# A one-core hybrid decoder layer: TensorE and the head's loads in program order, auxiliary bursts after counted turns, attention's products two turns behind its transposes

## The chip, the cores and the metric

The kernel runs on one core of one Trainium2 chip. The metric is the device time of one execution in microseconds (us). Before the change the timed runs took 1463.61 us in the median of three (1463.49 to 1464.78).

## The reference

One layer of a Hymba-style decoder on a sequence of 256 tokens of width 2048, all in float32. A normed input goes through one wide projection; its parts feed a Mamba-2 state-space branch (32 heads of 64, four groups of B and C) and a sparse attention branch (16 query heads of 128 over 4 groups of keys and values, with a compressed, a selected and a window part). Both are normed, go through one output projection, and a causal ConvFFN follows.

```python
h = rms_norm(x, mix_norm_w[l])
proj = h @ w_in[l]
z, xbc, dt_raw, q, kc, vc, ksl, vsl, kwn, vwn, gl = jnp.split(proj, split_at, axis=-1)
xbc = jax.nn.silu(causal_depthwise_conv(xbc, ssm_conv_w[l], ssm_conv_b[l]))
...
y_ssm = ssd_chunked(...)      # decay_in * (C B^T), times x * dt
y_ssm = rms_norm(y_ssm * jax.nn.silu(z), ssm_norm_w[l])
y_attn = rms_norm(nsa_attention(...), attn_norm_w[l])
x = x + jnp.concatenate([y_attn, y_ssm], axis=-1) @ w_out[l]
h = rms_norm(x, ffn_norm_w[l])
u = causal_depthwise_conv(h @ w_up[l], ffn_conv_w[l], ffn_conv_b[l])
gate, val = jnp.split(u, 2, axis=-1)
x = x + (jax.nn.silu(gate) * val) @ w_down[l]
return rms_norm(x, final_norm_w)
```

## The kernel before

All tokens fit into two tiles of 128 (NT = 2), so the time goes into passing the weights through TensorE once. The kernel is a list of **steps** of 512 KB of weights. For each step one DMA of the sync queue brings `raw` (L328, four buffers, RAWS); ScalarE rounds it to `whi` (L338); VectorE takes the rest, `wlo` (L344); TensorE then multiplies whi with the high and low part of the activations and wlo with the high part: 16 + 8 matmuls of 256 columns (L368, L372), or 8 + 4 of 512 columns where tokens are the rows (L403, L407). Activations are split in the same way, in `hcat` for the input projection, `ya` and `ys` for the output projection, `hcatf` for the up projection.

The steps run in this order: the input projection (PLAN; the word b is the B of the state space, c its C, dt the step sizes, x its inputs, then the keys and values kc, vc, ks, vs, kw, vw, the queries q and the gate z), the output projection (64 steps), the up projection and the down projection. In the input and up projection each four steps end in a `post`, the evacuation of their two PSUM banks (`u`, L386, multiplies with the root r1 of the norm, spread over the partitions as `gate`). There are four banks for steps and four for everything else.

What else is to be done is written as generators, the **auxiliary** work: the products of B and C (`cb_group`, L517), the transposes of dt (L460) and of xs (`make_xdt`, L547), the state-space heads, the compressed blocks, the four groups of the attention, the splitting of ya and ys, the transposes of x1 (L1024) and its root r2 (`make_r2`, L1051). They wait in one queue, `aux`. After each step the loop gives out a number of **turns** (`tick`): 2 per step for b to x, 1.5 where PLAN names no other rate (R_SSM), 1.45 for q and z. A turn runs the first generator to its next `yield`.

An attention group first makes scores and exponentials, then `norm` scales p on VectorE (L813), `trans` transposes a block of p on TensorE (L835) and copies it out of PSUM as `pt` with a high and a low part (ScalarE L94, VectorE L95), and `pv` multiplies it with v (L852 to L854), or with the compressed v (L848). In the code a product follows the transposes of the next block in the same turn.

What sets the order: calls through `V`, `A` and `T` (VectorE, ScalarE, TensorE) are held in program order only while `pin` is set, which is up to step 6; calls of the sync queue are not held. Everywhere else a scheduler may move an engine's instructions against each other, and it places auxiliary matmuls inside steps. In the head, x comes in four loads between the first raw loads, then the parameters (14 small loads, L238 to L250), then the other raw loads, four buffers in turn. Loads are asked for seven steps ahead (LOADS), weights prepared three steps ahead (AHEAD). Steps 0 to 2 also transpose x and split it; the squares of x, the root and its spreading follow steps 3, 4 and 6. `warm_up` issues matmuls on a tile of ones, WARM = 7 ahead of the first transposes and FILL = 4 ahead of the first step.

Of the kernel before, what the change touches and what calls it, by code (L numbers as in the profile page):

```python
# [10 lines left out]
F32 = mybir.dt.float32  # L11
# [8 lines left out]
NT = 2  # L20
# [22 lines left out]
def hymba_kernel(  # L43
# [34 lines left out]
    class Pinned:  # L78


        def __init__(self, eng):
            self.eng = eng

        def __getattr__(self, name):
            fn = getattr(self.eng, name)
            if not pin:
                return fn
            return lambda *a, **kw: tc.keep_in_program_order(fn(*a, **kw))  # L88

    pin = []  # L90
    V, A, T = Pinned(nc.vector), Pinned(nc.scalar), Pinned(nc.tensor)

# [140 lines left out]
    def load_params():  # L233
        def prow(srcs):
            pt = big(24 + len(prow_specs), [P, P], F32, f"prow{len(prow_specs)}")
            r = 0
            for s_ in srcs:
                nc.sync.dma_start(pt[r:r + s_.shape[0], :], s_)  # L238
# [4 lines left out]
        prow([ssm_conv_w[0].rearrange("j (r c) -> (j r) c", c=P), rows(ssm_conv_b[0])])  # L243
        prow([rows(ssm_norm_w[0]), rows(attn_norm_w[0]), rows(ffn_norm_w[0]), cmp_pos_k[0], cmp_pos_v[0]])
        for j in range(3):
            prow([rows(ffn_conv_w[0, j])])
        prow([rows(ffn_conv_b[0])])
        nc.sync.dma_start(dtb, ssm_dt_bias.rearrange("o h -> h o"))
        nc.sync.dma_start(nA, ssm_a_log.rearrange("o h -> h o"))
        nc.sync.dma_start(drow, ssm_d[0].partition_broadcast(P))  # L250

# [66 lines left out]
    def add_chunk(pieces, nk, ncol, mm, post=None, ticks=2, pre=None):  # L318

        kh = nk // 2  # L320
        for hf in range(2):
            s = Step()

            def load(hf=hf, s=s):
                raw = stage.tile([P, 1024], F32, tag="raw", name="raw", bufs=RAWS)
                s.raw = raw[:, :kh * ncol].rearrange("p (k c) -> p k c", k=kh)
                for dst, src in pieces(s.raw, hf * kh, kh):
                    nc.sync.dma_start(dst, src)  # L328

# [95 lines left out]
    def dt_softplus(t80):  # L425
# [28 lines left out]
        A.dma_start(acum_d, e)  # L454
        yield
        ps = aux_bank()
# [53 lines left out]

    def cb_group(g):
        if g % 2 == 0:
            cbt.append(big(29 + g // 2, [P, 2, 384], F32, f"cbt{g // 2}"))
        for st in range(2):
            ps = aux_bank()
            b_ = bc[g][:, 0, :, st * P:(st + 1) * P]
            T.matmul(ps, b_[:, 0], bc[g][:, 1], start=True, stop=False)  # L517
            T.matmul(ps[:, 256:512], b_[:, 1], bc[g][:, 1, 0], start=False, stop=True)
# [22 lines left out]
    def make_xdt(i):  # L541
        xd = big(16 + i, [P, NT, 512], F32, f"xdt{i}")
        xdt.append(xd)
        for t in range(NT):
            ps = aux_bank()
            for j in range(4):
                T.transpose(ps[:, j * P:(j + 1) * P], xs[i][:, j, t * P:(t + 1) * P], ident)  # L547
# [210 lines left out]
    def attention(g):  # L758
# [127 lines left out]
        yield  # L886
        exps(1, 1)
        yield
# [4 lines left out]
        a1 = trans(0, 1)  # L893
        exps(1, 2)
        yield
        a2 = trans(0, 2)
# [5 lines left out]
        pv(po, 0, 1, a1, True, False)  # L902
        yield
        pv(po, 0, 2, a2, False, False)
        prev = trans(1, 1)
        yield
        pv(po, 0, 0, a0, False, True)
        finish(po, 0)
        place_cmp(1)
        po = aux_bank()  # L910
        for b in (2, 3, 4, 0):
            nxt = trans(1, b)
            pv(po, 1, b - 1 if b else 4, prev, b == 2, False)
            prev = nxt
            yield
        pv(po, 1, 0, prev, False, True)
        finish(po, 1)
        yield
# [73 lines left out]
    def split_attn():  # L992
        rr["a"] = token_rsqrt(lambda t: asq[0][:, t * P:(t + 1) * P], "ra")
        yield
        for k in range(16):
# [6 lines left out]
    def split_ssm():  # L1002
        for k in range(16):
# [3 lines left out]
            if k % 2 == 1:  # L1007
                yield
        rr["s"] = token_rsqrt(lambda t: ssq[0][:, t * P:(t + 1) * P], "rs")
        yield  # L1010
# [5 lines left out]

    def transpose_x1(c):
        for kk in range(4):
            k = 4 * c + kk
# [8 lines left out]
    def wout_evac(c, part):  # L1028
        def evac(t, ps):
            sl = x1[c][:, t]  # L1030
            V.scalar_tensor_tensor(sl, ps, rr[part][:, t:t + 1], sl, op0=ALU.mult, op1=ALU.add)
            if part == "s":
                jk = tmp.tile([P, 512], F32, tag="w512", name="junk", bufs=1)
                A.activation(jk, sl, AF.Square, accum_out=xsq[:, t, c:c + 1])
                if t == 1:
                    aux.append(transpose_x1(c))
                    if c == 3:
                        drain()
                        aux.append(make_r2())
        return evac  # L1040

    r2bc = [None]

    def make_r2():
        tot = const.tile([P, NT], F32, name="x1ss")
        V.tensor_reduce(tot, xsq, axis=AX.X, op=ALU.add)
        r2 = rsqrt_mean(tot, NT, "r2")
        yield
        ps = aux_bank()
# [423 lines left out]
    for i in range(n):  # L1473
# [68 lines left out]
```

## Time and profile before

| | us |
|---|---|
| median of the timed runs | 1463.61 |
| profiled execution | 1462.45 |
| its span | 1460.7 |
| TensorE busy, input projection's start (0 to 40) | 35.53 of 40 |
| TensorE busy, 40 to 100 | 58.13 of 60 |
| TensorE busy, 480 to 500 | 19.32 of 20 |
| TensorE busy, 520 to 540 and 540 to 560 | 19.35 and 19.12 of 20 each |
| TensorE busy, up projection (760 to 1200) | 440.00 of 440 |

The span runs from the first to the last instruction; 1.75 us of the execution lie around it. In the timeline a row is a run of like instructions on one engine: start, length, engine, line and count, then in brackets how long the engine had stood still before it and which instruction let it go on. In the list of waits such times are summed by the pair of lines. L88 is the line of the helper that records pinned instructions, L94 and L95 the lines of `split`; "PEld" is the loading of matmul weights, "SPq" the sync queue.

### The profile page before, as it was taken

To read this page: it belongs to the slowest core of one execution; us is meant where nothing else is said; L and a number is where in the kernel's file an instruction comes from. 1 tells how busy PE (TensorE), PEld (TensorE's weight loads), DVE (VectorE), ACT (ScalarE), POOL (GpSimd) and SP (SyncE) were. 2 spreads that over 40 slices of the span, in tenths; PEclk is the share of its full clock that TensorE was granted. 3 is DMA by queue.
4 is the path that set the end of the run, shared out by engine and by line. 5 is a ranking of instruction groups with operands and counts; after the bars stand their busy time and mean duration, and the time that the engine had idled before them with its cause. 6 is when DMAs were issued, how large, how long until landed. Compare 5 with 4: busy or idle time off the path is not lost.

```text
span 1460.7 us, 26504 instructions
## 1 busy us (share of the span) xinstructions
PE 1440.9 (99%) x10512; PEld 1346.8 (92%) x10512; DVE 1103.5 (76%) x1733; ACT 844.2 (58%) x1281; POOL 3.6 (0%) x19
## 2 busy tenths in 40 slices
PE   8999999999999999999999999999999999999997
PEld 8999999989999998888899999999999998788886
DVE  7899699756898898555476776776767778878777
ACT  6666456555676697444455555555555556555554
POOL 0000000000000000000000000000000000000000
PEclk9999999999999999999999999999999999999999
DMA  8667668775444446566556566666666565565664
GB/s 257 172 199 221 179 201 247 219 233 174 145 148 128 148 156 202 189 189 195 189 176 201 191 192 197 196 193 195 195 191 199 190 194 192 194 212 187 204 200 144
DMA packets 222701, 278.77 MB, mean 191 GB/s; under 512 B 13177, under 2 KB 186865, under 8 KB 222449
## 3 DMA queue, kind: packets, MB, share of 16 engines
q1 hardware_dynamic: 220800, 272.59, 59.6%
q10 hardware_dynamic: 1776, 4.50, 0.9%
q8 instruction: 82, 1.34, 0.4%
q14 instruction: 43, 0.34, 0.1%
HBM read 274.92 MB, written 2.13 MB: 190 GB/s over the span
## 4 chain that ended last, share of the span: by engine, by line
PE 90%; DVE 5%; ACT 3%; issue 1%; DMA 1%; DVEq 0%; ACTq 0%
PE mm L368 36%; PE mm L372 18%; PE mm L403 10%; PE mm L407 5%; PE aux L1142 4%; PE mm L1142 3%; PE aux L1145 2%; PE mm L1145 2%; PE mm L88 1%; DVE wlo L344 1%; DVE wlo L1174 1%; PE aux L1191 1%; PE aux L1190 1%; PE aux L585 1%; PE aux L1192 1%
## 5 line engine op out<-in xcount | busy, mean ns | idle before, releaser
L338 ACT ACTIVATE whi<-raw 128x1024 fp32r<-128x1024 f32 x408 | 431.4, 1058 | 428.3 <-PE mm L368 263.6
L344 DVE TENSOR_TENSOR wlo<-raw,whi 128x1024 fp32r<-128x1024 f32 x408 | 496.8, 1219 | 220.2 <-ACT whi L338 214.6
L368 PE MATMUL mm<-hcatf,whi 128*128 128x256 f32 x2816 | 348.6, 276 | 0.0
L368 PEld LDWEIGHTS mm<-hcatf,whi 128*128 128x128 f32 x2816 | 332.6, 188 | 0.1
L368 PE MATMUL mm<-hcat,whi 128*128 128x256 f32 x2192 | 279.2, 279 | 1.9 <-DVE u L386 1.9
L368 PEld LDWEIGHTS mm<-hcat,whi 128*128 128x128 f32 x2192 | 265.2, 188 | 4.5 <-issue 2.5
L372 PE MATMUL mm<-hcatf,wlo 128*128 128x256 f32 x1408 | 188.2, 276 | 0.0
L372 PEld LDWEIGHTS mm<-hcatf,wlo 128*128 128x128 f32 x1408 | 172.7, 188 | 0.0
L372 PE MATMUL mm<-hcat,wlo 128*128 128x256 f32 x1096 | 148.0, 277 | 0.0
L372 PEld LDWEIGHTS mm<-hcat,wlo 128*128 128x128 f32 x1096 | 135.6, 188 | 0.1
L1168 ACT ACTIVATE whi<-raw 128x1024 fp32r<-128x1024 f32 x88 | 91.6, 1056 | 67.8 <-DVE raw L1223 20.6
L1174 DVE TENSOR_TENSOR wlo<-raw,whi 128x1024 fp32r<-128x1024 f32 x88 | 105.7, 1219 | 13.0 <-ACT whi L1168 11.8
L403 PE MATMUL mm<-whi,ya 128*128 128x512 f32 x256 | 65.5, 394 | 0.0
L386 DVE TENSOR_TENSOR u<-mm,bc 128x256 f32<-128x256 f32 x88 | 37.2, 424 | 36.9 <-PE mm L372 35.7
L1142 PE MATMUL aux<-whi,act 128*128 128x512 f32 x256 | 63.4, 390 | 0.8 <-ACT whi L1168 0.8
L403 PE MATMUL mm<-whi,ys 128*128 128x512 f32 x256 | 63.2, 389 | 0.0
L1142 PE MATMUL mm<-whi,act 128*128 128x512 f32 x232 | 58.4, 389 | 0.0
L1142 PEld LDWEIGHTS aux<-whi,act 128*128 128x128 f32 x256 | 47.9, 188 | 11.2 <-ACT whi L1168 1.3
L403 PEld LDWEIGHTS mm<-whi,ys 128*128 128x128 f32 x256 | 48.1, 188 | 10.0
L403 PEld LDWEIGHTS mm<-whi,ya 128*128 128x128 f32 x256 | 47.3, 188 | 9.3
L1142 PEld LDWEIGHTS mm<-whi,act 128*128 128x128 f32 x232 | 43.6, 188 | 9.0
L799 ACT ACTIVATE p<-p,nm 128x256 f32<-128x256 f32 (+2 forms) x96 | 37.7, 394 | 3.0 <-DVE nm L783 1.4
(392 smaller groups left out, 1690.7 us busy)
## 6 DMA issues: line engine op xcount, KB each, us to landing
raw<-in_w_up_dram SPq DMA_DIRECT2D x176, 512.0 KB, 4.5
raw<-in_w_in_dram SPq DMA_DIRECT2D x160, 512.0 KB, 3.7
raw<-in_w_down_dram SPq DMA_DIRECT2D x88, 512.0 KB, 5.0
raw<-in_w_out_dram SPq DMA_DIRECT2D x64, 512.0 KB, 4.8
acq<-acum_d ACTq DMA_DIRECT2D x8, 512.0 KB, 4.7
raw<-in_cmp_w_k_dram SPq DMA_DIRECT2D x8, 512.0 KB, 4.4
raw<-in_cmp_w_v_dram SPq DMA_DIRECT2D x8, 512.0 KB, 4.4
x<-in_x_dram SPq DMA_DIRECT2D x4, 512.0 KB, 6.6
```

Of the source, the lines that this page charges most:

```text
L338: A.activation(hv, s.raw, AF.Copy)
L344: V.tensor_tensor(lv, s.raw, s.w[0].bitcast(F32), op=ALU.subtract)
L368: T.matmul(st["ps"][c], hv[:, kl, c * P:(c + 1) * P], k_of(k)[:, hl], start=(k == 0 and hl == 0), stop=False)
L372: T.matmul(st["ps"][c], lv[:, kl, c * P:(c + 1) * P], k_of(k)[:, 0], start=False, stop=(k == nk - 1))
L386: V.tensor_tensor(u, ps, root, op=ALU.mult)
L403: T.matmul(st["ps"][t], act(k)[:, hl, t * P:(t + 1) * P], hv[:, kl], start=(k == 0 and hl == 0), stop=False)
L407: T.matmul(st["ps"][t], act(k)[:, 0, t * P:(t + 1) * P], lv[:, kl], start=False, stop=(k == nk - 1))
L799: A.activation(v_, v_, AF.Exp, bias=nm[t][:, h, b:b + 1], accum_out=sm[t][:, h, b:b + 1])
L1142: T.matmul(x_[2 * t + n], act(k)[:, hl, t * P:(t + 1) * P], hv[:, n], start=(first and kl == 0 and hl == 0), stop=False)
L1145: T.matmul(x_[2 * t + n], act(k)[:, 0, t * P:(t + 1) * P], lv[:, n], start=False, stop=(last and kl == 1))
L1168: A.activation(hv[:, 0:n], src()[:, 0:n], AF.Copy)
L1174: V.tensor_tensor(lv[:, 0:n], src()[:, 0:n], s.w[0].bitcast(F32)[:, 0:n], op=ALU.subtract)
```

## The change

TensorE is always held in program order (`T` with `always=True`), and the sync queue's raw and parameter loads while `pin` is set, which now begins ahead of the parameters. The parameter loads become a generator that is dealt out between raw loads 4 to 7. FILL is 2. The squares and the root of x both follow step 3, the root is spread after step 5, ahead of the parameters' transposes.

With program order, the place of a burst is where the code issues it, so the code moves them: `pause` lets a generator give back a counted number of turns first (WAIT). `cb_pair` issues the products of two groups as one burst; `make_xdt` all eight transposes at once; the attention keeps transposed blocks in `held` and takes their product two turns later. The root of the attention norm is taken inside `split_ssm` instead of at the start of `split_attn`; the root of x1 at the last evacuation of the output projection, and what is left in `aux` is drained three steps into the up projection instead of at that evacuation. R_SSM goes from 1.5 to 1.75 and the rate of q and z from 1.45 to 1.55.

```diff
-AHEAD, LOADS, WARM, FILL = 3, 7, 7, 4
+AHEAD, LOADS, WARM, FILL = 3, 7, 7, 2
-R_SSM = 1.5
-RATE = {"b": 2, "c": 2, "dt": 2, "x": 2, "ck": 1, "cv": 1, "q": 1.45, "z": 1.45}
+R_SSM = 1.75
+RATE = {"b": 2, "c": 2, "dt": 2, "x": 2, "ck": 1, "cv": 1, "q": 1.55, "z": 1.55}
+WAIT = {"bc": 7, "xdt": 6, "dt": 9, "x1": 2}
...
-            if not pin:
+            if not (pin or self.always):
...
-    V, A, T = Pinned(nc.vector), Pinned(nc.scalar), Pinned(nc.tensor)
+    V, A, T, S = Pinned(nc.vector), Pinned(nc.scalar), Pinned(nc.tensor, True), Pinned(nc.sync)
...
-                    nc.sync.dma_start(dst, src)
+                    S.dma_start(dst, src)
...
         A.dma_start(acum_d, e)
-        yield
+        yield from pause(WAIT["dt"])
...
+    def pause(n):
+        for _ in range(n):
+            yield
+
+    def cb_pair(g0):
+        yield from pause(WAIT["bc"])
+        cbt.append(big(29 + g0 // 2, [P, 2, 384], F32, f"cbt{g0 // 2}"))
+        todo = []
+        for g in (g0, g0 + 1):
+            for st in range(2):
+                ps = aux_bank()
+                b_ = bc[g][:, 0, :, st * P:(st + 1) * P]
+                T.matmul(ps, b_[:, 0], bc[g][:, 1], start=True, stop=False)
+                T.matmul(ps[:, 256:512], b_[:, 1], bc[g][:, 1, 0], start=False, stop=True)
+                todo.append((g, st, ps))
+        for g, st, ps in todo:
...
-            if which == 1:
-                aux.append(cb_group(g))
+            if which == 1 and c == 1:
+                aux.append(cb_pair(g0))
...
-        for t in range(NT):
-            ps = aux_bank()
+        yield from pause(WAIT["xdt"] if i < 3 else WAIT["xdt"] - 1)
+        banks = [aux_bank() for _ in range(NT)]
+        for t, ps in enumerate(banks):
             for j in range(4):
                 T.transpose(ps[:, j * P:(j + 1) * P], xs[i][:, j, t * P:(t + 1) * P], ident)
+        for t, ps in enumerate(banks):
...
+        held = deque()
+
+        def turn(t, blk_):
+            held.append((t, blk_, trans(t, blk_)))
+
+        def product():
+            t, blk_, r = held.popleft()
+            first = blk_ == 1
+            if first:
+                pos[t] = aux_bank()
+            pv(pos[t], t, blk_, r, first, blk_ == 0)
+            if blk_ == 0:
+                finish(pos[t], t)
+
+        pos = [None, None]
+        turn(0, 1)
         exps(1, 3)
         yield
-        po = aux_bank()
-        a0 = trans(0, 0)
+        turn(0, 2)
         norm(1, p1[1], [2, 3])
...
+        yield
+        for t, blk_ in ((0, 0), (1, 1), (1, 2), (1, 3), (1, 4), (1, 0)):
+            turn(t, blk_)
+            product()
+            if (t, blk_) == (1, 2):
+                place_cmp(1)
             yield
...
     def split_attn():
-        rr["a"] = token_rsqrt(lambda t: asq[0][:, t * P:(t + 1) * P], "ra")
-        yield
...
+            if k == 7:
+                rr["a"] = token_rsqrt(lambda t: asq[0][:, t * P:(t + 1) * P], "ra")
+                yield
...
-                        drain()
-                        aux.append(make_r2())
+                        aux.append(spread_r2(root_x1()))
...
+    steps[edge["up"] + 3].pre = drain
...
-    loads_to(5)
-    load_params()
     pin.append(1)
+    params = load_params()
+    for i, k in ((4, 4), (5, 5), (6, 14), (7, 0)):
+        loads_to(i)
+        for _ in range(k):
+            next(params, None)
...
         if i == 3:
-            square_x((2,))
-        elif i == 4:
-            square_x((3,))
+            square_x((2, 3))
             root_x()
         elif i == 5:
+            spread_root()
             make_params()
         elif i == 6:
-            spread_root()
             pin.clear()
```

Three places show what becomes of the order. First the sync queue in the head, from the raw load of step 5 on; `prow`, `dtb`, `nA` and `drow` are the parameters. Before:

```order
L328 DMA raw<-in_w_in_dram 128x4x256
L238 DMA prow_169<-in_cmp_pos_v_dram 32x128
L238 DMA prow_175<-in_ffn_conv_w_dram 88x128
L238 DMA prow_177<-in_ffn_conv_w_dram 88x128
L238 DMA prow_179<-in_ffn_conv_w_dram 88x128
L238 DMA prow_181<-in_ffn_conv_b_dram 88x128
L248 DMA dtb<-in_ssm_dt_bias_dram 32x1
L249 DMA nA<-in_ssm_a_log_dram 32x1
L250 DMA drow<-in_ssm_d_dram 128x32
L328 DMA raw<-in_w_in_dram 128x4x256 x14
```

After (L89 is now the helper's line for everything that is held in order):

```order
L89 DMA raw<-in_w_in_dram 128x4x256
L89 DMA prow_167<-in_ffn_norm_w_dram 16x128
L89 DMA prow_167<-in_cmp_pos_k_dram 32x128
L89 DMA prow_167<-in_cmp_pos_v_dram 32x128
L89 DMA prow_175<-in_ffn_conv_w_dram 88x128
L89 DMA prow_177<-in_ffn_conv_w_dram 88x128
L89 DMA raw<-in_w_in_dram 128x4x256
L89 DMA prow_181<-in_ffn_conv_w_dram 88x128
L89 DMA prow_183<-in_ffn_conv_b_dram 88x128
L89 DMA dtb<-in_ssm_dt_bias_dram 32x1
```

The raw load of step 6 stood behind all 14 parameter loads and now stands behind nine of them, ahead of the last five.

Second, TensorE at the first products of B and C; `bc` holds the split B and C, `hcat` the activations. Before:

```order
L368 MATMUL mm<-hcat_125,whi 128x256 x16
L372 MATMUL mm<-hcat_125,wlo 128x256
L517 MATMUL aux<-bc_140 128x512
L518 MATMUL aux<-bc_140 128x256
L517 MATMUL aux<-bc_140 128x512
```

After:

```order
L89 MATMUL mm<-hcat_125,whi 128x256 x16
L89 MATMUL mm<-hcat_125,wlo 128x256 x8
L89 MATMUL aux<-bc_140 128x512
L89 MATMUL aux<-bc_140 128x256
L89 MATMUL aux<-bc_140 128x512
```

The burst stood behind the first of the eight wlo matmuls of step 13 and now stands between steps 14 and 15, whole steps on both sides.

Third, TensorE in the last group of the attention, near the end of the input projection; p_ rows are transposes, `pt,v` rows products. Before:

```order
L368 MATMUL mm<-hcat_123,whi 128x256 x16
L372 MATMUL mm<-hcat_123,wlo 128x256 x8
L835 MATMUL aux<-ident,p_6040 128x128 x2
L835 MATMUL aux<-ident,p_6041 128x128 x2
L852 MATMUL aux<-pt,v_3862 128x512
L853 MATMUL aux<-pt,v_3862 128x512
L835 MATMUL aux<-ident,p_6040 128x128 x2
L835 MATMUL aux<-ident,p_6041 128x128 x2
L368 MATMUL mm<-hcat_124,whi 128x256 x3
L854 MATMUL aux<-pt,v_3862 128x512
```

After:

```order
L89 MATMUL mm<-hcat_126,whi 128x256 x16
L89 MATMUL mm<-hcat_126,wlo 128x256 x8
L89 MATMUL aux<-ident,p_6066 128x128 x2
L89 MATMUL aux<-ident,p_6067 128x128 x2
L89 MATMUL aux<-pt,vcmp 128x512
L89 MATMUL aux<-ident,p_6066 128x128 x2
L89 MATMUL aux<-ident,p_6067 128x128 x2
L89 MATMUL aux<-pt,v_3357 128x512 x3
L89 MATMUL mm<-hcat_123,whi 128x256 x16
L89 MATMUL mm<-hcat_123,wlo 128x256 x8
```

A product followed the transposes of the next block and was torn by matmuls of a step; now two bursts of transposes lie between a block's own transposes and its product, and the steps stand whole.

More of the change, by code (lines that the diff above doesn't have):

```diff
@@ L78, in hymba_kernel, with __init__ @@
     class Pinned:
-        def __init__(self, eng):
-            self.eng = eng
+        def __init__(self, eng, always=False):
+            self.eng, self.always = eng, always
         def __getattr__(self, name):
             fn = getattr(self.eng, name)
-            if not pin:
+            if not (pin or self.always):
                 return fn
@@ L237, in prow @@
             for s_ in srcs:
-                nc.sync.dma_start(pt[r:r + s_.shape[0], :], s_)
+                S.dma_start(pt[r:r + s_.shape[0], :], s_)
                 r += s_.shape[0]
+                yield
             prow_specs.append((pt, r))
         rows = lambda v: v.rearrange("(r c) -> r c", c=P)
-        prow([ssm_conv_w[0].rearrange("j (r c) -> (j r) c", c=P), rows(ssm_conv_b[0])])
-        prow([rows(ssm_norm_w[0]), rows(attn_norm_w[0]), rows(ffn_norm_w[0]), cmp_pos_k[0], cmp_pos_v[0]])
+        yield from prow([ssm_conv_w[0].rearrange("j (r c) -> (j r) c", c=P), rows(ssm_conv_b[0])])
+        yield from prow([rows(ssm_norm_w[0]), rows(attn_norm_w[0]), rows(ffn_norm_w[0]), cmp_pos_k[0], cmp_pos_v[0]])
         for j in range(3):
[L246 to L250, printed above, removed]
+            yield from prow([rows(ffn_conv_w[0, j])])
+        yield from prow([rows(ffn_conv_b[0])])
+        S.dma_start(dtb, ssm_dt_bias.rearrange("o h -> h o"))
+        yield
+        S.dma_start(nA, ssm_a_log.rearrange("o h -> h o"))
+        yield
+        S.dma_start(drow, ssm_d[0].partition_broadcast(P))
     def make_params():
@@ L509, in hymba_kernel @@
     cbt = []
[L511 to L514, printed above, removed]
-            ps = aux_bank()
-            b_ = bc[g][:, 0, :, st * P:(st + 1) * P]
-            T.matmul(ps, b_[:, 0], bc[g][:, 1], start=True, stop=False)
-            T.matmul(ps[:, 256:512], b_[:, 1], bc[g][:, 1, 0], start=False, stop=True)
+    def pause(n):
+        for _ in range(n):
+            yield
+    def cb_pair(g0):
[10 more added lines that the diff above has]
+        for g, st, ps in todo:
             rt = t256("rt")
@@ L543, in make_xdt @@
         xdt.append(xd)
-        for t in range(NT):
-            ps = aux_bank()
+        yield from pause(WAIT["xdt"] if i < 3 else WAIT["xdt"] - 1)
+        banks = [aux_bank() for _ in range(NT)]
+        for t, ps in enumerate(banks):
             for j in range(4):
                 T.transpose(ps[:, j * P:(j + 1) * P], xs[i][:, j, t * P:(t + 1) * P], ident)
+        for t, ps in enumerate(banks):
             V.tensor_tensor(xd[:, t].rearrange("p (h e) -> p h e", e=64), ps.rearrange("p (h e) -> p h e", e=64),
@@ L887, in attention @@
         exps(1, 1)
+        exps(1, 2)
         yield
@@ L892, in attention @@
         yat[g] = big(12 + g, [P, 4, L], F32, f"yat{g}")
-        a1 = trans(0, 1)
-        exps(1, 2)
-        yield
-        a2 = trans(0, 2)
+        held = deque()
[11 more added lines that the diff above has]
+        turn(0, 1)
         exps(1, 3)
         yield
-        po = aux_bank()
-        a0 = trans(0, 0)
+        turn(0, 2)
         norm(1, p1[1], [2, 3])
-        pv(po, 0, 1, a1, True, False)
         yield
-        pv(po, 0, 2, a2, False, False)
-        prev = trans(1, 1)
-        yield
[L907 to L917, printed above, removed]
+        for t, blk_ in ((0, 0), (1, 1), (1, 2), (1, 3), (1, 4), (1, 0)):
[3 more added lines that the diff above has]
+                place_cmp(1)
+            yield
+        product()
+        yield
+        yield
+        product()
         yield
@@ L992, in split_attn @@
     def split_attn():
-        rr["a"] = token_rsqrt(lambda t: asq[0][:, t * P:(t + 1) * P], "ra")
-        yield
         for k in range(16):
@@ L1008, in split_ssm @@
                 yield
+            if k == 7:
+                rr["a"] = token_rsqrt(lambda t: asq[0][:, t * P:(t + 1) * P], "ra")
+                yield
         rr["s"] = token_rsqrt(lambda t: ssq[0][:, t * P:(t + 1) * P], "rs")
@@ L1017, in transpose_x1 @@
     def transpose_x1(c):
+        yield from pause(WAIT["x1"])
         for kk in range(4):
@@ L1037, in evac, with root_x1, spread_r2 @@
                     if c == 3:
-                        drain()
-                        aux.append(make_r2())
+                        aux.append(spread_r2(root_x1()))
         return evac
     r2bc = [None]
-    def make_r2():
+    def root_x1():
         tot = const.tile([P, NT], F32, name="x1ss")
         V.tensor_reduce(tot, xsq, axis=AX.X, op=ALU.add)
-        r2 = rsqrt_mean(tot, NT, "r2")
-        yield
+        return rsqrt_mean(tot, NT, "r2")
+    def spread_r2(r2):
         ps = aux_bank()
```

## The prediction

> **What bounds the kernel now.** I read the page first, then the list of TensorE's waits, then the timeline of TensorE at each place that the change touches. The page:
>
> ```profile
> span 1460.7 us, 26504 instructions
> PE 1440.9 (99%) x10512; PEld 1346.8 (92%) x10512; DVE 1103.5 (76%) x1733; ACT 844.2 (58%) x1281; POOL 3.6 (0%) x19
> PE 90%; DVE 5%; ACT 3%; issue 1%; DMA 1%; DVEq 0%; ACTq 0%
> ```
>
> TensorE is busy for 1440.9 of 1460.7 us, and the chain that ends last lies 90% on it. So the change can win only where TensorE waits (19.8 us in all) or where a matmul takes longer than it must. What TensorE waits for, by the list of waits (total, times, longest):
>
> ```profile
> PE mm L368 <- DVE u L386: 1.9, 1, 1.9
> PE aux L835 <- DVE p L813: 1.3, 2, 0.7
> PE aux L517 <- DVE bc L95: 1.1, 2, 0.8
> ...
> PE aux L460 <- DVE dtw L451: 0.7, 1, 0.7
> ...
> PE aux L854 <- DVE pt L95: 0.5, 1, 0.5
> ...
> PE aux L88 <- DVE r_r L88: 0.3, 1, 0.3
> PE aux L852 <- ACT pt L94: 0.3, 1, 0.3
> ...
> PE aux L1051 <- DVE r_r L167: 0.2, 1, 0.2
> ```
>
> These eight rows, ten waits, are the ones at places where the change reorders work; together 6.3 us. The rows left out belong to the first 8 us and to the last stage, which the change leaves as they are. What a matmul costs where nothing is in its way shows in the timeline of TensorE (start, length, line, count):
>
> ```profile
> 740.36 1.98 PE L368 MATMUL mm<-hcatf,whi 128*128 128x256 f32 x16
> 742.18 1.07 PE L372 MATMUL mm<-hcatf,wlo 128*128 128x256 f32 x8
> 743.08 1.64 PE L368 MATMUL mm<-hcatf,whi 128*128 128x256 f32 x13
> ```
>
> From start to start, 16 matmuls take 1.82 us and 8 take 0.90: 0.113 us each, 2.72 us for a step of 24. The lengths in the rows (1.98, 1.07) overlap the next row, so a stall has to be read from starts. [...]
>
> **The change part by part.** *The head.* Rows of TensorE, VectorE, ScalarE and the sync queue:
>
> ```profile
> 27.47 0.67 PE L88 MATMUL aux<-ident,prow 120*128 120x120 f32 x6
> ...
> 31.78 2.08 PE L368 MATMUL mm<-hcat,whi 128*128 128x256 f32 x16
> 33.69 1.07 PE L372 MATMUL mm<-hcat,wlo 128*128 128x256 f32 x8
> 36.61 2.09 PE L368 MATMUL mm<-hcat,whi 128*128 128x256 f32 x16 [1.85 <-DVE u L386]
> ```
> ```profile
> 16.01 1.22 DVE L88 TENSOR_TENSOR wlo<-raw,whi 128x1024 fp32r<-128x1024 f32 x1
> ...
> 27.78 1.22 DVE L88 TENSOR_TENSOR wlo<-raw,whi 128x1024 fp32r<-128x1024 f32 x1
> ...
> 36.05 0.74 DVE L386 TENSOR_TENSOR u<-mm,gate 128x256 f32<-128x256 f32 x2
> ```
> ```profile
> 24.93 1.06 ACT L88 ACTIVATE whi<-raw 128x1024 fp32r<-128x1024 f32 x1 [3.92 <-DMA raw<-in_w_in_dram]
> 20.24 18.09 SPq L328 DMA_DIRECT2D raw<-in_w_in_dram x10
> ```
>
> Step 8 stands 1.85 us because its two banks are read (u, 36.05) only after the root r1 was spread. That chain begins with the weights of step 6: their load is issued at 20.24, behind eight parameter loads, though the buffer that it takes was free at 16.01 + 1.22 = 17.2. ScalarE meanwhile waits 3.92 us for it. With the parameter loads dealt out between the raw loads, the load goes out at about 17.2, 3.0 us sooner, and the evacuation can be at 33.0, before TensorE is through step 7 (33.69 + 8 x 0.113 = 34.6): the 1.9 goes. The spreading of the root moves up too, from after step 6 to after step 5, ahead of the parameter transposes. Its input, which the 0.3 row shows late at 31.34 (31.78 less the four transposes of 0.44), comes 3.0 us sooner, and another 1.2 because both squares now stand ahead of the split of step 7 (27.78): 27.1. TensorE is there at 27.47, so the fit is close; a wait of 0 to 0.9 is open, and I take 0. The five parameter loads that now stand behind the load of step 6 still go out around 20 us, as their last ones did, and are read after 27.47. Head: 2.2 us gained. Pinning the sync queue costs nothing of itself as long as the order written is the order of need, and it ends with step 6.
>
> The halved warm-up filler removes half of the first row below:
>
> ```profile
> 6.98 1.16 PE L88 MATMUL aux<-warm_t 128*128 128x128 f32 x8 [0.54 <-DVE hcat L88]
> 7.89 1.31 PE L88 MATMUL mm<-hcat,whi 128*128 128x256 f32 x9
> ```
>
> Eight records run from 6.98 to 7.89; four fewer are worth at most 0.46 us, and nothing if the step waits for its operands. VectorE and ScalarE prepare those at just this time, so I take 0.
>
> *Bursts placed by counted turns.* The products of B and C stood inside a step, before their operand was split:
>
> ```profile
> 54.87 0.28 PE L372 MATMUL mm<-hcat,wlo 128*128 128x256 f32 x1
> 55.96 0.47 PE L517 MATMUL aux<-bc 128*128 128x512 f32 x1 [0.82 <-DVE bc L95]
> ```
>
> They move behind the whole of the next step (2.7 us later, against a wait of 0.82 here and 0.3 at the second pair): 1.1 gained. The dt transposes move a step on as well, against a wait of 0.7: gained. Only auxiliary work reads either, and that work is moved back by more turns than they are. The transposes of xs were torn and stood a little early:
>
> ```profile
> 141.31 0.99 PE L368 MATMUL mm<-hcat,whi 128*128 128x256 f32 x7
> 142.35 0.44 PE L547 MATMUL aux<-ident,xs 128*128 128x128 f32 x2
> 142.54 0.36 PE L368 MATMUL mm<-hcat,whi 128*128 128x256 f32 x1
> 142.75 0.43 PE L547 MATMUL aux<-ident,xs 128*128 128x128 f32 x2
> ```
>
> Seven matmuls take 1.04 us where 0.79 is due, a stall of 0.25 that no list shows; and the one between the two pairs takes 0.21 instead of 0.113, 0.1 for being torn off. Bursts of eight have neither. Of eight such bursts (0 to 0.8 us for the tearing) I take half: 0.4.
>
> *Attention.* The transposes of p stood a turn ahead of the product, and the whole of TensorE's queue behind them:
>
> ```profile
> 484.58 1.19 PE L368 MATMUL mm<-hcat,whi 128*128 128x256 f32 x8
> 486.45 0.30 PE L835 MATMUL aux<-ident,p 128*128 128x128 f32 x1 [0.69 <-DVE p L813]
> ...
> 536.57 0.49 PE L835 MATMUL aux<-ident,p 128*128 128x128 f32 x3
> 537.71 0.30 PE L835 MATMUL aux<-ident,p 128*128 128x128 f32 x1 [0.65 <-DVE p L813]
> ```
>
> With whole steps in between and the products two turns behind, the copies (pt) have a step of 2.72 us more, so the 0.3 and 0.5 for pt go; the two waits for p (1.3) hang on VectorE's norm and go only where the burst lands later than it did. Listed: 2.1. At the end of the input projection, the moved root of the attention norm takes its column sums out of the first step of the output projection:
>
> ```profile
> 558.28 0.48 PE L403 MATMUL mm<-whi,ya 128*128 128x512 f32 x1
> 558.80 0.38 PE L989 MATMUL aux<-ones,asq 128*128 128x1 f32 x2
> ```
>
> One matmul of 512 columns takes 0.52 instead of 2 x 0.113: 0.29 more, again unlisted. The last part, r2 a step later, gains the listed 0.2; its drain moves three steps into the up projection, where a step is 2.72 us as anywhere.
>
> *Tails.* Each listed wait stands longer from start to start than the list says: step 8 stood 36.61 - 34.60 = 2.01 (listed 1.85), the B and C product 0.98 (0.82), the p transposes 0.97 (0.69) and 0.80 (0.65). The commonest excess is 0.16; for ten waits, 1.6 us.
>
> *What is given back.* The last group's waits (0.65 for p, 0.3 and 0.5 for pt, each with its tail: 1.9) have no later group to hide behind, and its norms keep their place among the weight splits. Bounds 0 and 1.9; I keep 1.0. New waits: TensorE no longer takes what is ready but what is next. The ends are 0 and, were each of 32 transposing bursts late, 32 x 0.97 = 31; nearest are the two at hand, so I put in two of 0.69: 1.4.
>
> *Sum.* 2.2 + 1.1 + 0.7 + 2.1 + 0.2 = 6.3 listed; + 1.6 tails + 0.5 unlisted (0.25 and 0.29) + 0.4 tearing = 8.8; less 1.0 and 1.4: **6.4 us**. The profiled execution took 1462.45 us (its span 1460.7 and 1.75 around it), so 1456.05. The median shown, 1463.61, is 1.16 above that execution; on its footing **1457.2**.
>
> **The rivals.** *VectorE becomes the bound.* Two stages:
>
> ```profile
> 180.00:260.00 80.00, 80.00 (x660) 74.72 (x657) 77.69 (x134) 47.77 (x56) 0.00 (x0) 1.00 0.73 225
> ...
> 560.00:740.00 180.00, 180.00 (x821) 149.28 (x821) 101.08 (x123) 85.44 (x108) 0.00 (x0) 1.00 0.60 191
> ```
>
> (Busy us of TensorE, weight loads, VectorE, ScalarE, GpSimd; then clock.) In the SSM stretch VectorE has 2.3 us left of 80. Weight splits take at most 80 / 2.72 x 1.22 = 36 of its 77.7; the other 42 come in turns, and 1.75 turns a step instead of 1.5 bring 17% more of them, 7.0 us. Less the 2.3, VectorE falls 4.7 us behind. Weights are prepared three steps ahead (8 us), and TensorE did not wait once there, so I price it at 0 in the sum; as a rival, with the lead used up, all 4.7 come through: **1461.9**. Chance 0.10.
>
> *The waits only stay.* If p and the root are late by their engines' own work and not by their place, the attention's 2.1 and the head's 2.2 remain with their tails; what goes is 1.1 + 0.7 + 0.2 and four tails (0.6), with 0.5 and 0.4: 3.5, less 1.4 new: **1461.5**. For it: the p waits name VectorE, which had a weight split ahead of the norm. Against: the head's row names a load that was held back in the queue. Chance 0.11.
>
> *In order, TensorE stops for late bursts (slower).* A transposing burst of the attention that comes before its norm is done holds all 24 matmuls of the next step behind it, 0.97 us each time as at 486.45; before, such a burst could be filled in with matmuls of the step, as at 484.58. It cancels the gain from nine of the 32 bursts and is slower by over 0.2% (2.9 us, about what a measurement of this kernel can tell from no change) from twelve: (8.8 + 2.9) / 0.97. With sixteen, two groups of four: 15.5 lost, **1470.3**. Against it: the mean lead grows. Chance 0.09.
>
> *The clock drops at the start.* The fewer filler matmuls leave TensorE idle for longer around 7 us. The window there:
>
> ```profile
> 6.00:8.00 2.00, 1.46 (x13) 1.22 (x12) 1.09 (x6) 1.98 (x6) 0.00 (x0) 1.00 1.06 396
> ```
>
> The granted clock is 1.00 with 0.54 us idle; at half rate, one step of 2.72 us and some of the next, say 1.7 us more in all, would give **1458.9**. Chance 0.03. [...]
>
> **How the numbers follow.** Forecast 0.67, VectorE 0.10, waits stay 0.11, late bursts 0.09, clock 0.03. Faster by over 0.2% (under 1460.7): 0.67 + 0.03 = 0.70; within: 0.10 + 0.11 = 0.21; slower 0.09. The low end: nothing given back, filler and tearing in full (8.8 + 0.46 + 0.4 = 9.7), and, since after a burst 16 matmuls take 1.91 (31.78 to 33.69) instead of 1.82, 0.1 in each of up to 20 steps that stand behind one burst less: 11.7, 1452. The high end takes in the two rivals near 1462: 1463. Some 0.08 is left out below and 0.09 above.
>
> **What would show it.** Right: no wait at step 8 and the load of step 6 out near 17 us; no row for bc or dtw in the list of waits; steps whole, at 2.72 us; p waits in the last group alone. Wrong: TensorE idle between 180 and 260 us behind a weight split; waits for p or pt in every group, of about 0.7 each; a wait for r_r at 27.5 above 0.9; a sum of TensorE's busy time that does not fall while its waits do.

## The result, and the profile after

| | before | after |
|---|---|---|
| median of the timed runs, us | 1464.19 (1463.49 to 1465.37, 4 runs) | 1454.45 (1453.97 to 1455.43, 4 runs) |
| profiled execution, us | 1462.45 | 1454.14 |
| its span, us | 1460.7 | 1452.4 |

The ratio after to before is 0.9934, with a 95% interval of 0.9916 to 0.9951: the change makes the kernel 0.66% faster, 9.7 us between the medians and 8.3 us between the profiled executions. The forecast was 6.4 us.

The page of the changed kernel, the same lines as before:

```profile
span 1452.4 us, 26500 instructions
PE 1437.5 (99%) x10508; PEld 1346.9 (93%) x10508; DVE 1101.5 (76%) x1733; ACT 844.7 (58%) x1281; POOL 3.6 (0%) x19
PE 93%; DVE 3%; ACT 2%; DMA 1%; issue 1%; DVEq 0%; ACTq 0%
```

TensorE is still the engine that sets the end; its busy time fell by 3.4 us and its idle time from 19.8 to 14.9. The list of what TensorE waits for is now five rows long:

```profile
PE aux L89 <- DVE p L827: 2.4, 3, 1.1
PE aux L89 <- ACT whi L1193: 1.2, 1, 1.2
PE aux L89 <- DVE sqrt_set L119: 1.1, 1, 1.1
PE aux L89 <- DMA x<-in_x_dram: 0.6, 1, 0.6
PE mm L89 <- DVE wlo L1199: 0.6, 1, 0.6
```

All but the first lie in the first 8 us and in the last stage, as before. Of the ten waits that the prediction listed, only those for p stay, and they grew: from 1.3 us in two places to 2.4 in three. The busy time by stages (TensorE first after the length):

```profile
40.00:100.00 60.00, 60.00 (x517) 59.37 (x517) 52.96 (x105) 39.88 (x66) 0.00 (x0) 1.00 0.61 175
...
180.00:260.00 80.00, 80.00 (x631) 73.34 (x631) 78.36 (x137) 50.26 (x63) 0.00 (x0) 1.00 0.73 221
...
400.00:480.00 80.00, 78.51 (x652) 76.73 (x652) 70.93 (x133) 62.48 (x159) 0.00 (x0) 1.00 0.48 139
...
520.00:540.00 20.00, 19.06 (x156) 18.21 (x155) 18.79 (x37) 19.91 (x42) 0.00 (x0) 1.00 0.46 145
```

Between 40 and 100 us TensorE now has no gap (58.13 of 60 before). Between 180 and 260 VectorE is busy for 78.36 of 80 us, more than before, and TensorE still does not wait. The gaps left are at 476 to 478 and at 530 us.

Since both kernels do the same weight steps in the same order, the start of a step's first matmul in the timeline tells where the time went. Each difference is after less before:

| start of | before | after | difference | gained since the row above |
|---|---|---|---|---|
| step 12 (the head done) | 47.61 | 45.62 | -1.99 | 1.99 |
| step 53 (products of B and C, dt, xs done) | 171.07 | 164.76 | -6.31 | 4.32 |
| step 122 (state-space heads, compressed blocks done) | 348.85 | 342.90 | -5.95 | -0.36 |
| step 182 (attention done, output projection begun) | 569.93 | 561.80 | -8.13 | 2.18 |
| step 250 (x1, r2 and the drain done) | 760.35 | 751.94 | -8.41 | 0.28 |

Three matmuls of the attention's scores (0.38 us) stand ahead of step 122 after the change (six from 342.15) and behind it before (three from 348.48). Without them the state-space row is 0.02 and the attention's 1.80. Behind step 250 nothing more changes: the spans differ by 8.3.

### The profile page after: what moved, and what is told of

It is laid out like the page before. It is cut to its first block, busy times and chain, and to the rows that moved or that the text cites. A ratio compares the mean times of both kernels' runs of the same rounds, so it can differ in the third digit from the quotient of the medians.

```text
span 1452.4 us, 26500 instructions
## 1 busy us (share of the span) xinstructions
PE 1437.5 (99%) x10508; PEld 1346.9 (93%) x10508; DVE 1101.5 (76%) x1733; ACT 844.7 (58%) x1281; POOL 3.6 (0%) x19
## 4 chain that ended last, share of the span: by engine, by line
PE 93%; DVE 3%; ACT 2%; DMA 1%; issue 1%; DVEq 0%; ACTq 0%
PE mm L89 80%; PE aux L89 13%; DMA raw<-in_w_down_dram 1%; DVE wlo L1199 1%; ACT p L813 1%; DMA x<-in_x_dram 0%; DVE wlo L348 0%; ACT whi L342 0%; DVE p L789 0%; ACT whi L1193 0%; DVE x L1395 0%; ACT L813 0%; ACT junk L1354 0%; DVE p L827 0%; ACT acc L962 0%
## 5 line engine op out<-in xcount | busy, mean ns | idle before, releaser
L89 PE MATMUL mm<-hcatf,whi 128*128 128x256 f32 x2816 | 348.3, 276 | 0.0
L89 PEld LDWEIGHTS mm<-hcatf,whi 128*128 128x128 f32 x2816 | 332.6, 188 | 0.1
L89 PE MATMUL mm<-hcat,whi 128*128 128x256 f32 (+1 forms) x2336 | 295.4, 278 | 0.0
L89 PEld LDWEIGHTS mm<-hcat,whi 128*128 128x128 f32 (+1 forms) x2336 | 281.7, 188 | 2.6 <-issue 0.7
L89 PE MATMUL mm<-hcatf,wlo 128*128 128x256 f32 x1408 | 188.3, 276 | 0.0
L89 PEld LDWEIGHTS mm<-hcatf,wlo 128*128 128x128 f32 x1408 | 172.8, 188 | 0.0
L89 PE MATMUL mm<-hcat,wlo 128*128 128x256 f32 (+1 forms) x1168 | 159.7, 277 | 0.0
L89 PEld LDWEIGHTS mm<-hcat,wlo 128*128 128x128 f32 (+1 forms) x1168 | 144.4, 187 | 0.2 <-DVE wlo L89 0.2
L1199 DVE TENSOR_TENSOR wlo<-raw,whi 128x1024 fp32r<-128x1024 f32 x88 | 105.8, 1220 | 12.9 <-ACT whi L1193 11.7
L89 PE MATMUL aux<-whi,act 128*128 128x512 f32 (+1 forms) x306 | 77.9, 387 | 1.2 <-ACT whi L1193 1.2
L89 PE MATMUL mm<-whi,act 128*128 128x512 f32 (+1 forms) x286 | 74.1, 386 | 0.0
L89 PEld LDWEIGHTS aux<-whi,act 128*128 128x128 f32 x306 | 57.0, 188 | 13.2 <-ACT whi L1193 1.5
L89 PE MATMUL mm<-whi,ya 128*128 128x512 f32 x256 | 64.3, 393 | 0.0
L89 PEld LDWEIGHTS mm<-whi,act 128*128 128x128 f32 x286 | 53.5, 188 | 11.1
L89 PE MATMUL mm<-whi,ys 128*128 128x512 f32 x256 | 63.2, 389 | 0.0
L89 PEld LDWEIGHTS mm<-whi,ys 128*128 128x128 f32 x256 | 48.1, 188 | 10.0
L89 PEld LDWEIGHTS mm<-whi,ya 128*128 128x128 f32 x256 | 47.5, 188 | 9.7
L89 PE MATMUL aux<-wlo,act 128*128 128x512 f32 (+1 forms) x153 | 43.7, 388 | 0.0
```

The costliest lines, as they stand in the source:

```text
L1199: V.tensor_tensor(lv[:, 0:n], src()[:, 0:n], s.w[0].bitcast(F32)[:, 0:n], op=ALU.subtract)
```

## The experiments

Each time is a median beside the median of the kernel before in the same comparison (1462.67, 1463.1 and 1463.74 us in the three); the intervals are those of the ratio to it. The stage behind step 250, which no run changes, takes between 700.2 and 702.7 us in the 14 profiles, so small differences are read from the starts of steps ahead of it and not from one execution's time.

**The order without program order.** The changed kernel, TensorE held only up to step 6:

```diff
-    V, A, T, S = Pinned(nc.vector), Pinned(nc.scalar), Pinned(nc.tensor, True), Pinned(nc.sync)
+    V, A, T, S = Pinned(nc.vector), Pinned(nc.scalar), Pinned(nc.tensor), Pinned(nc.sync)
```

> The changed kernel with TensorE held in program order only up to step 6, as before the change; every counted turn stays. Theory 'place' (the gain comes from where the code issues the bursts): the order stays nearly what it was, so 1454.5 us within 1, ratio to before 0.993. Rival 'order' (holding TensorE in program order is what keeps steps whole): the 2 to 3 us gained around the products of B and C, dt and xs are lost, 1457 us or more.

Measured: 1453.22 us, ratio 0.9935 (0.992 to 0.995). Given the new places in the code, the scheduler leaves them: TensorE's order differs from the changed kernel's in one place, in the attention, where it puts two matmuls of the step and some products ahead of the late transposes. There it wins 1.2 us (steps 122 to 182 take 217.71 us instead of 218.90). Steps 53 and 122 start 0.29 us sooner, no more than the 0.29 by which step 1 already came sooner. So holding TensorE in program order gains nothing by itself.

**Program order without the new places.** The kernel before, TensorE always held:

```diff
-            if not pin:
+            if not (pin or self.always):
...
-    V, A, T = Pinned(nc.vector), Pinned(nc.scalar), Pinned(nc.tensor)
+    V, A, T = Pinned(nc.vector), Pinned(nc.scalar), Pinned(nc.tensor, True)
```

> The kernel before with TensorE always held in program order and nothing else changed. Theory 'place': bursts stand where the old code issues them, right behind the evacuation that feeds them, so TensorE waits for their operands: not faster than before, 1464 us or slower, with waits for bc, dt and xs of about 1 us each and more of them. Rival 'order': steps are whole again, 2 to 3 us faster, 1461 us.

Measured: 1527.89 us, ratio 1.0444 (1.0428 to 1.0459): 65 us slower. The direction was that of the theory, but it had put the waits at about 1 us each, and they are 4 to 8. TensorE's waits in this kernel:

```profile
PE aux L88 <- ACT xs L601: 16.9, 4, 5.2
PE aux L88 <- DVE bc L95: 12.0, 2, 6.6
PE aux L88 <- DVE dtw L451: 7.6, 1, 7.6
PE aux L88 <- DVE r_r L167: 3.9, 1, 3.9
```

A burst that the code issues in the turn right behind the evacuation waits 4 to 8 us for the chain through ScalarE and VectorE, with the whole queue behind it. The scheduler had hidden this in the kernel before by moving bursts back, though not always far enough.

**Program order and whole bursts without the counts.**

```diff
-WAIT = {"bc": 7, "xdt": 6, "dt": 9, "x1": 2}
+WAIT = {"bc": 0, "xdt": 1, "dt": 1, "x1": 0}
```

> The changed kernel with every counted wait taken out (bc 0, xdt 1, dt 1, x1 0 turns), the bursts otherwise as changed. Theory 'place': the waits for bc, dt and xs come back, and larger than before since no matmul is put in between: 3 to 6 us slower than the changed kernel, 1457.5 to 1460.5. Rival 'burst' (one burst instead of several is what counts): within 1 us of 1454.5.

Measured: 1514.48 us, ratio 1.035 (1.0333 to 1.0367), 60 us slower than the changed kernel, ten times the 3 to 6 that the theory expected. The waits are those of the run above (16.9 for xs, 12.3 for bc, 7.6 for dtw). So the counts are what program order needs to be harmless, and the rival that the burst alone counts falls.

**The counts without program order.** The kernel before, with `pause`, `cb_pair`, `make_xdt` and the dt wait of the change and nothing else:

```diff
+WAIT = {"bc": 7, "xdt": 6, "dt": 9}
...
-            if which == 1:
-                aux.append(cb_group(g))
+            if which == 1 and c == 1:
+                aux.append(cb_pair(g0))
```

> The kernel before with the counted turns and whole bursts for the products of B and C, for dt and for xs alone; nothing pinned beyond step 6. Theory 'place': the waits for bc and dtw and the torn xs bursts go without any program order, steps 13 to 53 come 4.3 us sooner against step 12 than in the kernel before (as in the changed kernel: 3.3 to step 35, 1.0 to step 53), of which the prediction's terms priced 2.95; since the turns are used up, later work may come later and give some back, 1459 to 1462 us. Rival 'order': without program order the scheduler moves them back, within 0.5 us at step 53.

Measured: 1458.86 us, ratio 0.9967 (0.9956 to 0.9979). From step 12 to step 53 it takes 119.51 us (47.72 to 167.23) where the kernel before takes 123.46 and the changed one 119.14: 3.95 of the 4.32 us come from the counts and whole bursts alone. What the burst of B and C looks like after the change:

```profile
52.87 1.07 PE L89 MATMUL mm<-hcat,wlo 128*128 128x256 f32 x8
53.78 1.56 PE L89 MATMUL aux<-bc 128*128 128x512 f32 x8
55.17 1.98 PE L89 MATMUL mm<-hcat,whi 128*128 128x256 f32 x16
56.99 1.07 PE L89 MATMUL mm<-hcat,wlo 128*128 128x256 f32 x8
57.90 1.98 PE L89 MATMUL mm<-hcat,whi 128*128 128x256 f32 x16
```

and what stood behind it before:

```profile
58.24 2.05 PE L368 MATMUL mm<-hcat,whi 128*128 128x256 f32 x16
60.13 1.10 PE L372 MATMUL mm<-hcat,wlo 128*128 128x256 f32 x8
61.06 2.05 PE L368 MATMUL mm<-hcat,whi 128*128 128x256 f32 x16
```

The stall is gone, and also something that followed it: before, 16 matmuls behind the burst take 1.89 us from start to start (58.24 to 60.13), after 1.82 (55.17 to 56.99).

**The attention's products one turn behind.** The changed kernel with the attention's turns as before, exponentials and norms in their old turns too:

```diff
-        turn(0, 1)
-        exps(1, 3)
-        yield
-        turn(0, 2)
-        norm(1, p1[1], [2, 3])
+        a1 = trans(0, 1)
+        exps(1, 2)
+        yield
+        a2 = trans(0, 2)
+        exps(1, 3)
...
+        for b in (2, 3, 4, 0):
+            nxt = trans(1, b)
+            pv(po, 1, b - 1 if b else 4, prev, b == 2, False)
+            prev = nxt
+            yield
```

> The changed kernel with the attention's turns as they were: each product one turn behind its transposes, exponentials and norms in their old turns, in program order. Theory 'lag' (a product needs the copies of its transposes, 0.58 us on ScalarE and 0.68 on VectorE behind a weight split of 1.2): waits for pt of 0.3 to 0.8 in most of 32 products, 3 to 8 us slower than the changed kernel, 1457.5 to 1462.5. Rival (only p was late, and one turn is enough): within 1 us of 1454.5, with the same waits for p.

Measured: 1463.48 us, ratio 1.0005 (0.9995 to 1.0014): the whole gain is gone again, 9 us against the changed kernel, more than expected. Waits for pt come back, but only three of them (3.1 us) where the theory had most of 32 products, and the largest wait is one for p; behind it TensorE runs at half speed:

```profile
470.82 0.33 PE L89 MATMUL aux<-ident,p 128*128 128x128 f32 x1 [0.61 <-DVE p L827]
473.47 0.45 PE L89 MATMUL aux<-ident,p 128*128 128x128 f32 x1 [2.32 <-DVE p L827]
473.57 3.76 PE L89 MATMUL mm<-hcat,whi 128*128 128x256 f32 x16
477.13 1.91 PE L89 MATMUL mm<-hcat,wlo 128*128 128x256 f32 x8
```
```profile
473.00:476.00 3.00, 2.53 (x12) 2.56 (x13) 2.87 (x5) 0.60 (x1) 0.00 (x0) 0.50 0.69 193
476.00:479.00 3.00, 3.00 (x16) 3.00 (x15) 0.07 (x1) 1.06 (x1) 0.00 (x0) 0.51 0.46 155
```

The step takes 5.27 us (473.57 to 478.84) instead of 2.72, and the granted clock, the number after the busy times, reads 0.50. The run does not part the lag from the moved exponentials and norms; it shows what the new arrangement of the attention as a whole is worth in program order.

**The head, one half at a time.** First the parameter loads ahead of the load of step 6 again:

```diff
-    for i, k in ((4, 4), (5, 5), (6, 14), (7, 0)):
+    for i, k in ((4, 6), (5, 14), (6, 0), (7, 0)):
```

> The changed kernel with the raw load of step 6 behind all 14 parameter loads again. Theory 'load' (the head's gain is that load going out 2 us sooner): the root comes 2 to 3 us later and its spreading, now in order ahead of step 6, waits for it: steps from 8 on are 2 to 3 us later than in the changed kernel, 1456.5 to 1457.5 us. Rival 'root' (the earlier squares and spreading make the gain): within 0.5 us of it up to step 8.

Measured: 1456.23 us, ratio 0.9955 (0.994 to 0.9969). Step 8 starts at 36.78, no sooner than in the kernel before (36.61); TensorE waits 2.7 us for r_r, ahead of step 6 instead of ahead of step 8. Then squares, root and spreading at their old places:

```diff
-            square_x((2, 3))
+            square_x((2,))
+        elif i == 4:
+            square_x((3,))
             root_x()
         elif i == 5:
-            spread_root()
             make_params()
         elif i == 6:
+            spread_root()
             pin.clear()
```

> The changed kernel with squares, root and spreading after steps 3, 4 and 6 as before, the loads dealt out as changed. Theory 'load': the root has 1 to 2 us to spare, no wait comes back, within 0.5 us of the changed kernel, 1454.5. Rival 'root': the wait at step 8 comes back by 1 us or more.

Measured: 1456.02 us, ratio 0.995 (0.9935 to 0.9964), and the wait at step 8 is back in its old size:

```profile
35.84 2.10 PE L89 MATMUL mm<-hcat,whi 128*128 128x256 f32 x16 [1.85 <-DVE u L390]
```

My theory had this run wrong. With the loads dealt out, the five last parameter loads stand ahead of the load of step 7, which goes out no sooner than before (21.30, before 20.91), and the old order puts the second square behind the split of its weights (27.00, before 27.78): the root's last step is at 30.25 us (31.03 before), against 26.93 in the run with one turn of lag, whose head is that of the changed kernel. Either half alone gains little (step 8 at 36.78 and 35.84, before 36.61); both together gain 2.8 (33.84 in that run).

**The turns per step as before.**

```diff
-R_SSM = 1.75
-RATE = {"b": 2, "c": 2, "dt": 2, "x": 2, "ck": 1, "cv": 1, "q": 1.55, "z": 1.55}
+R_SSM = 1.5
+RATE = {"b": 2, "c": 2, "dt": 2, "x": 2, "ck": 1, "cv": 1, "q": 1.45, "z": 1.45}
```

> The changed kernel with the turns per step as before (1.5 and 1.45). Rival 'VectorE' (1.75 turns overload VectorE between 180 and 260 us): up to 4.7 us faster there. Theory 'room' (the higher rates cost nothing there and bring the last attention group in before the output projection drains the queue): no gain between steps 56 and 110, and 1 to 5 us lost at the start of the output projection, 1455.5 to 1459.5.

Measured: 1458.79 us, ratio 0.9971 (0.9961 to 0.9981), 4 us slower than the changed kernel by the medians. From step 56 to 110 it takes 135.45 us, the changed kernel 135.98: the higher rate costs 0.5 there at most, not 4.7. The loss is where it was expected, at the drain ahead of the output projection: step 177 starts 8.0 us sooner than in the changed kernel (work was left over) and step 182 5.3 us later, with waits of 3.11 for pt and 1.64 for the placed p (pc), and a clock of 0.68 between 550 and 560 us.

**The filler.** The changed kernel with the old one:

```diff
-AHEAD, LOADS, WARM, FILL = 3, 7, 7, 2
+AHEAD, LOADS, WARM, FILL = 3, 7, 7, 4
```

> The changed kernel with FILL 4. [...] Rival 'filler': step 1 at 11.6 in every profile with FILL 4, and the median 0.5 to 1 us faster, 1453.7.

Measured: 1455.19 us, ratio 0.9945 (0.9931 to 0.9958), and step 1 at 12.91 us. It answers a question that the profile of the changed kernel raised. Its first rows, and those of the run with one turn of lag, which has the same head:

```profile
5.29 1.97 PE L89 MATMUL aux<-ident,x 128*128 128x128 f32 x8 [0.60 <-DMA x<-in_x_dram]
7.06 1.22 PE L89 MATMUL aux<-warm_t 128*128 128x128 f32 x4
7.94 2.99 PE L89 MATMUL mm<-hcat,whi 128*128 128x256 f32 x16
10.76 1.03 PE L89 MATMUL aux<-ident,x 128*128 128x128 f32 x8
```
```profile
5.23 1.09 PE L89 MATMUL aux<-ident,x 128*128 128x128 f32 x8 [0.58 <-DMA x<-in_x_dram]
6.87 0.71 PE L89 MATMUL aux<-warm_t 128*128 128x128 f32 x4 [0.54 <-DVE hcat L89]
7.46 2.46 PE L89 MATMUL mm<-hcat,whi 128*128 128x256 f32 x16
9.75 1.04 PE L89 MATMUL aux<-ident,x 128*128 128x128 f32 x8
```

The eight transposes take 1.97 us in the one and 1.09 in the other. In the first, matmuls stand 0.213 us apart up to 9.8 us; in the second, half of that from 5.2 us on. This is decided before the filler is reached, and of the 14 profiles of this study seven have the late form, with step 1 at 12.3 to 12.9 us (12.57 in the first here), and seven the early one, at 11.4 to 11.7 (11.56 in the second). With FILL 4 both occur: early in the kernel before (11.69), late here. So the filler is not the cause (what decides the form was not shown), and the profiled execution of the changed kernel lost 0.9 us that the profiled execution of the kernel before did not.

**Towards a better version.** The waits left are those for p at the first transposes of the second token tile. One turn more ahead of them:

```diff
         turn(0, 2)
         norm(1, p1[1], [2, 3])
         yield
+        yield
```

> The changed kernel with one turn more between the attention's second transposes and the rest, so that the norm of the second token tile has 1.75 us more. Theory 'norm' (the remaining waits for p, 2.4 us in three places, come from that norm standing one turn too close): they go, 2 to 3 us faster up to step 177, and some of it may come back where the output projection drains the queue: 1452 to 1454. Rival (VectorE is simply behind there): the waits move with the burst, within 0.5 us of 1454.5.

Measured: 1454.73 us, ratio 0.9944 (0.9929 to 0.9959). The waits for p go and step 177 starts at 542.20 instead of 547.27, but more turns are left at the drain: step 178 starts 8.90 us behind step 177 (2.96 in the changed kernel), after waits for pt of 0.7, 0.7 and 0.6, and all is given back. Two ways to make room were tried on top. More turns for q and z:

```diff
-RATE = {"b": 2, "c": 2, "dt": 2, "x": 2, "ck": 1, "cv": 1, "q": 1.55, "z": 1.55}
+RATE = {"b": 2, "c": 2, "dt": 2, "x": 2, "ck": 1, "cv": 1, "q": 1.65, "z": 1.65}
```

> The changed kernel with the extra turn ahead of the attention's later transposes and 1.65 turns per step for q and z. Theory 'norm' with 'room': the waits for p go as in the run with the extra turn (up to 5 us gained to step 177) and the last group is through before the output projection drains the queue: 1450 to 1452 us. Rival: VectorE and ScalarE cannot do more per step there, waits for pt or p come back elsewhere, 1454 to 1456.

Measured: 1453.85 us, ratio 0.9938 (0.9926 to 0.9951), with one wait for p of 1.1 us back: nothing beyond the changed kernel. And one of the two empty turns at the end of a group taken out:

```diff
         product()
         yield
-        yield
         product()
```

> The changed kernel with the extra turn ahead of the attention's later transposes and one of the two empty turns at the group's end taken out, rates as changed. Theory 'room': no more turns per group than in the changed kernel, so the output projection drains no more than there: 1450 to 1452.5 us. Rival: the last product, one turn after its transposes, waits where it is drained, 1 to 2 us: 1453 to 1455.

Measured: 1452.18 us (1450.59 to 1453.07, 5 runs), ratio 0.9923 (0.9911 to 0.9936). One wait is left between 100 and 700 us:

```profile
PE aux L89 <- DVE pt L96: 1.3, 1, 1.3
```

From step 122 to 182 it takes 217.18 us, the changed kernel 218.90 (218.7 to 218.9 in the five profiles with its attention and its rates): 1.7 us gained. Its interval overlaps that of the changed kernel (0.9916 to 0.9951), so that it beats it is shown by the profile of that stretch, not by the times.

## Why the prediction was right

**The bound and the list of waits.** Right: what was gained lies at the places that the eight rows named, and the up projection did not change. Reading the list as a sum of 6.3 us was too low a count, as the next points show: with starts alike, the profiled gain is 9.2 us (8.3 and the 0.9 of the filler's paragraph) against 6.4. The prediction did not part program order from the new places; the runs do, and the gain is the places'.

**The head, 2.2 and its tails of 0.3.** The wait at step 8 is gone and step 12 comes 1.99 us sooner, 2.89 where the half speed ended early (47.61 to 44.72, in the run with one turn of lag). The load of step 6 goes out at 18.29 (17.87 there), 2.0 to 2.4 us sooner and not 3.0. The working was incomplete at one step: I gave the load 3.0 us and the order of the squares 1.2. The two half-experiments show that neither is worth much alone, since with the loads moved and the old order the second square waits behind the split of step 7.

**Filler at 0.** Nearly right: where the half speed ends early, step 1 starts at 11.40 to 11.56 with FILL 2 and at 11.53 to 11.69 with FILL 4, some 0.1 us.

**Products of B and C, dt, xs: 1.1 + 0.7, with tails of 0.5, 0.25 and 0.4, together 2.9.** Measured 4.32, of which the counts alone bring 3.95. The waits went, but one step of the working was wrong. Counted in the steps of the table above, the first burst had stood inside step 14, not 13, behind its first wlo matmul. So it moved behind seven matmuls, 0.8 us, and not behind a whole step of 2.7, and it had waited 0.98 from start to start. The rest came from VectorE, whose order nothing holds there. Before:

```profile
53.07 2.41 DVE L344 TENSOR_TENSOR wlo<-raw,whi 128x1024 fp32r<-128x1024 f32 x2
55.40 0.75 DVE L95 TENSOR_TENSOR bc<-acc,bc 128x256 fp32r<-128x256 f32 x2
```

After:

```profile
51.47 1.21 DVE L348 TENSOR_TENSOR wlo<-raw,whi 128x1024 fp32r<-128x1024 f32 x1
52.60 0.75 DVE L96 TENSOR_TENSOR bc<-acc,bc 128x256 fp32r<-128x256 f32 x2
```

One weight split less stands ahead of the split of bc, which starts 1.54 us behind the start of step 14 (51.06) instead of 2.35 (53.05). In the run with the counts alone VectorE's order is the old one, and 0.19 us of the wait is left (the matmul ahead of the burst starts at 55.77 and the burst at 56.07, 0.30 us apart where 0.113 is due).

The size was too low. The 936 weight matmuls of 256 columns in this stretch take 111.17 us from start to start before and 106.76 after. Five stops make 2.8 us of that, near the 2.95 of the terms; the other 1.6 is matmuls that are a little slow. I had used the 0.119 of the head's row only to widen the range.

**VectorE as the bound (1461.9).** Did not come: with 1.75 turns VectorE was busy for 78.36 of 80 us and TensorE waited for nothing, and the run with the old rates gains 0.5 there.

**Attention, 3.0 with tails less 2.4 given back, 0.6 net.** Measured 2.18, or 1.80 without the three score matmuls that changed sides of step 122. Both sides were too low: in the kernel before, the stretch from step 122 to 182 holds 3.9 us of stops from start to start in eight places, where the list names 2.1 in four; after, 3.0 in three. So the stops gave 0.9, and slow or torn matmuls about as much. The part that I gave back, waits for p, is what the list still shows, though at the second-to-last group as much as at the last.

**The last part, 0.4 with its tail.** 0.28.

**Late bursts stop TensorE (1470.3).** Did not come in the changed kernel, but the mechanism is real: without the counts it costs 60 us, at the bursts of xs, B and C and dt rather than at the attention. I had looked for it in the attention and priced it at 15.5. That the change is safe from it hangs on the counted turns, and at the end of the attention on the rates: with the old ones 4 us are lost there.

**The clock at the start (1458.9).** The half speed was seen, up to 9.8 us and with step 1 at 12.57 instead of 11.69, but is no matter of the filler. No run shows the 1.7 us that this rival was priced at; the two starts lie 0.88 us apart.

## What to carry over

In this kernel, program order on the saturated engine gained nothing by itself and took away the scheduler's repair of bursts issued too early; the gain lay in issuing a burst some steps behind the evacuation that feeds it, whole, and the scheduler then left it there. Count the turns from the chain that feeds the burst, and count what is left in the queue at the next drain too, because a turn added in one place is paid there. Read stalls from start to start and price the slow matmuls behind them: in the attention the list of waits held 2.1 of the 3.9 us of stops.

## What the runs showed of the hardware

In three runs a stall of TensorE cost more than its length. In the run with one turn of lag, after 0.61 and 2.32 us of idling within 3.7 us (469.83 to 473.57), matmuls of 256 columns stood 0.22 us apart for 5.3 us; the granted clock reads 0.85 from 470 to 473 us, 0.50 and 0.51 in the next two stretches of 3 us, and 1.00 from 479 to 482. In the kernel with program order alone, the clock reads 0.66 between 50 and 60 us, where a wait of 6.61 us ends at 54.45. In the run with the old rates, with waits of 3.11 and 1.64 us, it reads 0.81 from 540 to 550 and 0.68 from 550 to 560. Single waits of up to 1.13 us in the changed kernel did not do this (1.00 from 400 to 480), nor did one of 2.7 us in the run with the raw load of step 6 behind all parameter loads, whose mean clock is 0.998 like that of the changed kernel (0.996 in the run with one turn of lag). What decides between these cases was not shown.

The granted clock in the windows did not show the half speed at the start: between 6 and 11 us it reads 1.00 in each us of both kernels, though matmuls of 256 columns stand 0.213 us apart up to 9.8 us in the changed one and 0.118 in the kernel before, and only the distance of the starts tells it.

Behind the stall at the first products of B and C in the kernel before (58.24 to 62.95), and behind the small transposes of dt in the changed kernel (95.74 to 101.46), matmuls of 256 columns stood 0.118 to 0.119 us apart for about two steps instead of 0.113, and then went back at once. From step 122 to 182 two in five stand so, at 0.116 to 0.124, in both kernels (507 of the 1286 that another one follows before, 510 of 1297 after). What brings and ends it stayed open; no run was made for it.
